# A larger head piece in a free strip buffer and a last group in three parts, in a DMA-bound diagonal prefix-sum kernel

## The chip, the cores and the metric

The kernel runs on one core of one Trainium2 chip. The metric is device time in microseconds (us), the median of several executions. All executions told here are of the fast state. A ratio is the mean time of one kernel's fast runs over the mean of the other's of the same rounds on the same chip, so it is not quite the ratio of the medians quoted beside it. Its 95% interval is given in brackets. Different sets of rounds ran on different chips.

## The reference

```python
def setup_inputs():
    B, H, W = 4, 4224, 4224
    return {"x": np.random.randn(B, H, W).astype(np.float32)}

def reference(x):
    ps = np.cumsum(np.cumsum(x, axis=1), axis=2)
    diag = np.diagonal(ps, axis1=1, axis2=2)
    return np.cumsum(diag, axis=1).astype(np.float32)
```

Every element of x has to be read once: 4 x 4224 x 4224 floats, 285 MB. The output is tiny.

## The kernel before: what the change touches

Rows are handled in groups of 384. Most of x is loaded in strips of 768 rows (6 rows on each of 128 partitions) by casting transfers, f32 to bf16, issued from GpSimd. There are three strip buffers. TensorE adds the columns right of the diagonal, VectorE (DVE) and ScalarE (ACT) the rows left of it. The last group of the last batch is loaded in pieces, so that little work is left when the last byte lands. A "head" of it, the last 528 columns of its first 256 rows, is loaded right at the start through the hardware queue in f32, while the casting queue gets going.

```python
    HC = 528
    src_a = x[LB, T0:TB, :].rearrange("(h p) w -> p h w", p=P)
    head = last.tile([P, 2, HC], FP32, name="head")
    nc.sync.dma_start(out=head, in_=src_a[:, :, N - HC : N])
    ...                                           # strips: pool "strips", bufs=NBUF (3)
    prefetched = []
    for i in range(NBUF):
        t = strip_tile()
        load_rows(t, 0, i * F2 * P)
        prefetched.append(t)
    ...                                           # batch loop; last batch only, after its last strips:
            part_a = strip[:, 0:2]                # 2 x 128 rows, without the head's columns
            part_b = strip[:, 2]                  # the last 128 rows
            acuts = [(1536, N - HC), (0, 1536)]
            bcuts = [(2432, TB), (640, 2432), (0, 640)]
            ...                                   # five casting transfers; first piece of a is folded here
        ...                                       # pu, carry, two scans (c12), output of the other groups
        fold_in(fold_a, part_a, c0, cp, 256)      # second piece of a
        ...
        row_sums(arows, asum)
        for i, ((c0, c1), (wp, wa)) in enumerate(zip(bcuts, shares)):
            fold_in(fold_b, part_b, c0, c0 + wp, 256, start=i == 0)
            ...
            if i == 0:
                matmul(fin_b, arows[:, 0:1], weights[:, 2 * P : GW], start=True)
                matmul(fin_b, arows[:, 1:2], weights[:, P : 2 * P])
                matmul(fin_a, arows[:, 0:1], weights[:, 0 : 2 * P], start=True)
                matmul(fin_a[:, P : 2 * P], arows[:, 1:2], weights[:, 0:P])
        row_sums(ttot, tsum)
        matmul(fin_b, ttot, weights[:, 0:P])
```

`fold_in` is a chain of matmuls with the identity that add columns of bf16 data into one bank of PSUM, the memory that TensorE writes to. The names that matter in the tail: `d` holds what each position of the diagonal adds, `pu` the sums of `d` by group, `arows` the row sums of part a (256 rows), `tsum` and `ttot` those of part b (128 rows). "The last add" is DVE's last instruction, which makes the last 128 results. I call the four products with `arows` "the fin products". In the program the fold of the middle piece of part b stands behind them, and in the trace it runs behind them (661.37, 661.80, then 662.64).

## Time and profile before

| | before |
|---|---|
| median of the first runs | 669.56 us (668.67 to 670.19) |
| span of the profiled execution | 667.0 us |
| casting queue, share of the 16 DMA engines' span | 99.7% |
| busiest compute engine | DVE, 50% |

A timeline line has the start and the length in us, the engine, the source line, the operation, output<-input, shape and count. What stands in brackets is the idle time ahead of it and what ended that. The lines themselves are shown in the prediction.

### The profile page before, as it was taken

Reading aid. Unit: us, or ns where it says so; the run is one execution under the profiler, and the core shown is the slowest. Engines: PE = TensorE matmul, PEld = TensorE weight load, DVE = VectorE, ACT = ScalarE, POOL = GpSimd, SP = SyncE. Lnnn points to the kernel's source line nnn. Section 1 sums busy time; section 2 is a strip of 40 time slices with the busy share of each in tenths; the row PEclk is TensorE's granted clock in tenths of the full one; section 3 lists DMA queues with packets and bytes.
Section 4 is the critical chain, followed back from the end, with each engine's and each line's share of the span. In section 5 each row is a group of like instructions: output and inputs, shape, how many; then the busy total and the mean of one; then the engine's idle time right before and its main releaser. Section 6 shows DMA issues by size and latency. Waiting matters only on the chain.

```text
span 667.0 us, 2828 instructions
## 1 busy us (share of the span) xinstructions
PE 215.1 (32%) x967; PEld 97.2 (15%) x967; DVE 336.3 (50%) x376; ACT 140.1 (21%) x225; POOL 27.0 (4%) x56
## 2 busy tenths in 40 slices
PE   0071522403118254140321633504032254250426
PEld 0030211101003022010110311201011122120202
DVE  2043617366924351745883415266398241635687
ACT  0001120406300103040630020304063002030436
POOL 5000000000000000000000000000000000001000
PEclk9995857666558586665655957567565586765758
DMA  9999999999999999999999999999999999999997
GB/s 203 219 219 219 218 219 219 217 217 216 208 215 219 219 219 217 216 219 219 219 219 215 216 211 217 220 219 216 216 216 219 220 215 218 216 215 219 216 207 144
DMA packets 7384, 143.25 MB, mean 215 GB/s; under 512 B 669, under 2 KB 842, under 8 KB 1866
## 3 DMA queue, kind: packets, MB, share of 16 engines
q0 software_dynamic: 7008, 142.47, 99.7%
q1 hardware_dynamic: 362, 0.61, 0.3%
q8 instruction: 7, 0.11, 0.1%
q14 instruction: 7, 0.06, 0.0%
HBM read 285.47 MB, written 0.07 MB: 428 GB/s over the span
## 4 chain that ended last, share of the span: by engine, by line
another core or an unknown queue 42%; DVE 25%; PE 23%; DMA 5%; issue 4%; DVEq 0%; POOLq 0%
PE d L198 23%; DVE acc L215 17%; DVE mu L218 7%; DMA strip<-in_x_dram 5%; PE fold L198 1%; DVE pu L215 0%; DVE c L397 0%; DVE c L218 0%; DVE tsum L215 0%; DVE acc L301 0%; DVE acc L304 0%; PE carry_ps L198 0%; DVE rows L331 0%; DVEq L218 0%
## 5 line engine op out<-in xcount | busy, mean ns | idle before, releaser
L218 DVE SCALAR_TENSOR_TENSOR mu<-strip,um 128x768 bf16<-128x768 bf16 (+1 forms) x129 | 110.7, 908 | 314.4 <-DMA strip<-in_x_dram 222.3
L198 PE MATMUL d<-strip,sel 128*11 128x384 bf16 x603 | 140.0, 406 | 344.4 <-DMA strip<-in_x_dram 344.4
L210 ACT ACTIVATE dump<-strip 128x416 bf16<-128x416 bf16 (+8 forms) x112 | 128.4, 1146 | 523.2 <-DMA strip<-in_x_dram 520.2
L215 DVE TENSOR_REDUCE acc<-strip 128x6 f32<-128x4608 bf16 (+6 forms) x23 | 195.9, 8518 | 0.0
L198 PEld LDWEIGHTS <-sel 128*11 128x11 bf16 x849 | 86.1, 101 | 526.3 <-issue 488.4
L198 PE MATMUL d<-mu,sel 128*11 128x384 bf16 x243 | 59.7, 355 | 67.5 <-DVE mu L218 67.4
L75 POOL DMA_DIRECT2D strip<-in_x_dram x24 | 16.5, 687 | 555.5 <-DVE acc L215 414.5
L210 ACT ACTIVATION_READ_ACCUMULATOR dump<-strip 128x1 f32 x112 | 20.9, 186 | 0.0
L218 DVE DVE_READ_ACCUMULATOR mu<-strip,um 128x1 f32 x129 | 10.6, 82 | 0.0
L198 PE MATMUL d<-ident,rows 128*11 128x128 f32 x24 | 5.2, 378 | 16.5 <-DVE rows L340 16.5
L198 PE MATMUL fold<-strip,ident_h 128*128 128x480 bf16 (+1 forms) x14 | 4.3, 458 | 8.4 <-DMA strip<-in_x_dram 8.4
L198 PE MATMUL d<-halves,rows 128*11 128x64 f32 x48 | 5.7, 304 | 0.0
L198 PEld LDWEIGHTS d<-halves,rows 128*11 128x11 f32 x48 | 5.1, 136 | 2.1 <-issue 2.1
L198 PEld LDWEIGHTS d<-ident,rows 128*11 128x11 f32 x24 | 2.6, 118 | 18.2 <-DVE rows L340 11.5
L215 DVE TENSOR_REDUCE pu<-d 11x1 f32<-11x384 f32 x4 | 2.2, 546 | 5.5 <-PE d L198 5.5
L397 DVE TENSOR_TENSOR_SCAN c<-ones_row,carry,c 11x384 f32<-11x384 f32 x4 | 4.0, 1006 | 0.1
L397 DVE TENSOR_TENSOR_SCAN c<-ones_row,carry,d 11x384 f32<-11x384 f32 x4 | 4.0, 1001 | 0.1
L198 PEld LDWEIGHTS <-ident_h 128*128 128x128 bf16 x20 | 2.2, 112 | 12.2 <-issue 11.8
L215 DVE TENSOR_REDUCE parts<-strip 128x3 f32<-128x3072 bf16 x1 | 3.4, 3350 | 0.0
L198 PE MATMUL d<-hmu,sel 128*11 128x384 bf16 (+2 forms) x3 | 0.7, 286 | 6.7 <-DVE hmu L218 6.7
L372 POOL DMA_DIRECT2D strip<-in_x_dram x2 | 1.4, 716 | 29.2 <-DVE acc L215 29.2
L215 DVE TENSOR_REDUCE tsum<-strip 128x1 f32<-128x384 bf16 (+2 forms) x3 | 1.7, 568 | 0.9 <-DMA strip<-in_x_dram 0.9
(78 smaller groups left out, 36.0 us busy)
## 6 DMA issues: line engine op xcount, KB each, us to landing
strip<-in_x_dram POOLq DMA_DIRECT2D x19, 6336.0 KB, 69.6
strip<-in_x_dram POOLq DMA_DIRECT2D x5, 3168.0 KB, 55.3
strip<-in_x_dram POOLq DMA_DIRECT2D x1, 1080.0 KB, 45.3
strip<-in_x_dram POOLq DMA_DIRECT2D x1, 768.0 KB, 48.2
head<-in_x_dram SPq DMA_DIRECT2D x1, 528.0 KB, 3.9
strip<-in_x_dram POOLq DMA_DIRECT2D x1, 448.0 KB, 51.1
strip<-in_x_dram POOLq DMA_DIRECT2D x1, 416.0 KB, 49.5
strip<-in_x_dram POOLq DMA_DIRECT2D x1, 160.0 KB, 51.4
```

The source lines that it names most:

```text
L75: nc.gpsimd.dma_start(out=o, in_=x[b, r0 : r0 + f * P, :].rearrange("(p f) w -> p f w", f=f))
L198: nc.tensor.matmul(o, lhsT=lhsT, rhs=rhs, start=start, stop=False, skip_group_check=True)
L210: nc.scalar.activation(out=dump[:, :w], in_=src, func=ACT.Copy, accum_out=acc)
L215: nc.vector.reduce_sum(out=acc, in_=src, axis=AX.X)
L218: nc.vector.scalar_tensor_tensor(out=o, in0=i, scalar=1.0, in1=m, op0=ALU.mult, op1=ALU.mult, accum_out=acc,)
L372: nc.gpsimd.dma_start(out=part_a[:, :, c0:c1], in_=src_a[:, :, c0:c1])
L397: nc.vector.tensor_tensor_scan(out=c12[:, i, :], data0=ones_row, data1=src, initial=carry[:, i : i + 1], op0=ALU.mult, op1=ALU.add,)
```

## The change

The intent, as the diff reads, is to load more of the last group early and in longer contiguous runs (8448 bytes), to put it into a strip buffer that is still free, and to leave less for the end, each part of 128 rows being handled by itself. The core of the diff:

```diff
-    HC = 528
-    src_a = x[LB, T0:TB, :].rearrange("(h p) w -> p h w", p=P)
-    head = last.tile([P, 2, HC], FP32, name="head")
-    nc.sync.dma_start(out=head, in_=src_a[:, :, N - HC : N])
+    HC = N // 2
+    HP2 = 2 * P
...
+    head = strips.tile([P, F, N], FP32, name="strip")[:, 0, :HC]
+    nc.sync.dma_start(out=head, in_=x[LB, T0 : T0 + P, N - HC : N])
     prefetched = []
-    for i in range(NBUF):
+    for i in range(NBUF - 1):
...
-                diag_b = last.tile([P, P], BF16, name="diag_b")
-                nc.gpsimd.dma_start(out=diag_b, in_=x[b, TB:N, TB:N])
+                ends = last.tile([P, 2, HP2], BF16, name="ends")
+                nc.gpsimd.dma_start(
+                    out=ends,
+                    in_=x[b, T0 + P : N, N - HP2 : N].rearrange("(h p) w -> p h w", p=P),
+                )
...
-            wp, ws = 1280, 1280 + 1536
+            wp, ws = 1440, 1440 + 1440
...
-            acuts = [(1536, N - HC), (0, 1536)]
-            bcuts = [(2432, TB), (640, 2432), (0, 640)]
+            apieces = [(0, 0, N - HC, 1024), (1, 1536, N - HP2, 1280), (1, 0, 1536, 768)]
+            bpieces = [(2176, N - HP2), (640, 2176), (0, 640)]
...                     # the fin products stay between the first and the second fold of part b
+        fold_in(fold_b, src, c0, c0 + 768, 256, start=True)
+        act_sum(tsum[:, 1:2], src[:, c0 + 768 : c1])
+        matmul(fin_b, arows[:, 0:1], weights[:, 2 * P : GW], start=True)
+        matmul(fin_b, arows[:, 1:2], weights[:, P : 2 * P])
+        matmul(fin_a, arows[:, 0:1], weights[:, 0 : 2 * P], start=True)
+        matmul(fin_a[:, P : 2 * P], arows[:, 1:2], weights[:, 0:P])
+        fold_in(fold_b, src, c2, c2 + 768, 256)
...
```

More of the change, by code (lines that the diff above doesn't have):

```diff
@@ L239 @@
         nc.vector.memset(rows3[i], 0.0)
-    asum = last.tile([P, 2, 5], FP32, name="asum")
-    tsum = last.tile([P, 8], FP32, name="tsum")
+    asum = last.tile([P, 2, 4], FP32, name="asum")
+    tsum = last.tile([P, 7], FP32, name="tsum")
     hs = last.tile([P, 3], FP32, name="hs")
@@ L246 @@
     hmu = last.tile([P, 3, GW], BF16, name="hmu")
-    row_sums(hs[:, 0:2], head)
-    for h in range(2):
-        w = GW - h * P
-        masked(hmu[:, h, :w], head[:, h, HC - w : HC], um1[:, :w], hu[:, h : h + 1])
-    nc.vector.tensor_sub(out=asum[:, :, 0], in0=hs[:, 0:2], in1=hu[:, 0:2])
+    row_sums(hs[:, 0:1], head)
+    masked(hmu[:, 0, :], head[:, HC - GW : HC], um1, hu[:, 0:1])
+    nc.vector.memset(asum, 0.0)
     for b in range(B):
@@ L315 @@
             if not whole and s == 0:
-                diag_b = last.tile([P, P], BF16, name="diag_b")
-                nc.gpsimd.dma_start(out=diag_b, in_=x[b, TB:N, TB:N])
-            if not whole and s == 1:
-                row_sums(hs[:, 2:3], diag_b)
-                masked(hmu[:, 2, :P], diag_b, um1[:, :P], hu[:, 2:3])
-                nc.vector.tensor_sub(
-                    out=tsum[:, 0:1], in0=hs[:, 2:3], in1=hu[:, 2:3]
-                )
+                ends = last.tile([P, 2, HP2], BF16, name="ends")
[3 more added lines that the diff above has]
+                )
+            if not whole and s == 1:
+                row_sums(hs[:, 1:3], ends)
+                for h in range(2):
+                    w = (2 - h) * P
+                    masked(
+                        hmu[:, h + 1, :w],
+                        ends[:, h, HP2 - w :],
+                        um1[:, :w],
+                        hu[:, h + 1 : h + 2],
+                    )
+                nc.vector.tensor_sub(out=asum[:, :, 0], in0=hs[:, 0:2], in1=hu[:, 0:2])
+                nc.vector.tensor_sub(out=tsum[:, 0:1], in0=hs[:, 2:3], in1=hu[:, 2:3])
                 for h in range(3):
@@ L365, with a_piece @@
         if not whole:
-            strip = strip_tile()
-            part_a = strip[:, 0:2]
-            part_b = strip[:, 2]
-            acuts = [(1536, N - HC), (0, 1536)]
-            for c0, c1 in acuts:
-                nc.gpsimd.dma_start(out=part_a[:, :, c0:c1], in_=src_a[:, :, c0:c1])
-            bcuts = [(2432, TB), (640, 2432), (0, 640)]
-            for c0, c1 in bcuts:
-                nc.gpsimd.dma_start(out=part_b[:, c0:c1], in_=x[b, TB:N, c0:c1])
-            fold_a = psum_s.tile([P, 2, 256], FP32, name="fold_a")
-            c0, c1 = acuts[0]
-            cp, ca = c0 + 768, c0 + 768 + 1152
-            fold_in(fold_a, part_a, c0, cp, 256, start=True)
-            for h in range(2):
-                act_sum(asum[:, h, 1:2], part_a[:, h, cp:ca])
-            row_sums(asum[:, :, 2], part_a[:, :, ca:c1])
+            parts_l = strip_tile()
+            apieces = [(0, 0, N - HC, 1024), (1, 1536, N - HP2, 1280), (1, 0, 1536, 768)]
+            for h, c0, c1, _ in apieces:
+                r0 = T0 + h * P
+                nc.gpsimd.dma_start(
+                    out=parts_l[:, h, c0:c1], in_=x[b, r0 : r0 + P, c0:c1]
+                )
+            bpieces = [(2176, N - HP2), (640, 2176), (0, 640)]
+            for c0, c1 in bpieces:
+                nc.gpsimd.dma_start(out=parts_l[:, 2, c0:c1], in_=x[b, TB:N, c0:c1])
+            fold_a = psum_s.tile([P, 2, 256], FP32, name="fold_a")
+            def a_piece(n, start):
+                h, c0, c1, wp = apieces[n]
+                src = parts_l[:, h]
+                fold_in(fold_a[:, h], src, c0, c0 + wp, 256, start=start)
+                act_sum(asum[:, h, 1 + n // 2 : 2 + n // 2], src[:, c0 + wp : c1])
+            a_piece(0, True)
         pu = smalls.tile([NG, 2], FP32, name="pu")
@@ L411 @@
             continue
-        c0, c1 = acuts[1]
-        cp = c0 + 768
-        fold_in(fold_a, part_a, c0, cp, 256)
-        for h in range(2):
-            act_sum(asum[:, h, 3:4], part_a[:, h, cp:c1])
-        row_sums(asum[:, :, 4], fold_a)
+        a_piece(1, False)
+        a_piece(2, False)
+        row_sums(asum[:, :, 3], fold_a)
         arows = last.tile([P, 2], FP32, name="arows")
@@ L426 @@
         fin_b = psum_s.tile([1, P], FP32, name="fin_b")
-        shares = [(768, 512), (768, 512), (0, 320)]
-        n = 1
-        for i, ((c0, c1), (wp, wa)) in enumerate(zip(bcuts, shares)):
-            fold_in(fold_b, part_b, c0, c0 + wp, 256, start=i == 0)
-            act_sum(tsum[:, n : n + 1], part_b[:, c0 + wp : c0 + wp + wa])
-            if i == 2:
-                row_sums(tsum[:, n + 2 : n + 3], fold_b)
-            row_sums(tsum[:, n + 1 : n + 2], part_b[:, c0 + wp + wa : c1])
-            n += 2
-            if i == 0:
-                matmul(fin_b, arows[:, 0:1], weights[:, 2 * P : GW], start=True)
-                matmul(fin_b, arows[:, 1:2], weights[:, P : 2 * P])
-                matmul(fin_a, arows[:, 0:1], weights[:, 0 : 2 * P], start=True)
-                matmul(fin_a[:, P : 2 * P], arows[:, 1:2], weights[:, 0:P])
+        src = parts_l[:, 2]
+        (c0, c1), (c2, c3), (c4, c5) = bpieces
+        fold_in(fold_b, src, c0, c0 + 768, 256, start=True)
[5 more added lines that the diff above has]
+        fold_in(fold_b, src, c2, c2 + 768, 256)
+        act_sum(tsum[:, 2:3], src[:, c2 + 768 : c2 + 768 + 384])
+        row_sums(tsum[:, 3:4], src[:, c2 + 768 + 384 : c3])
+        act_sum(tsum[:, 4:5], src[:, c4 : c4 + 320])
+        row_sums(tsum[:, 5:6], fold_b)
+        row_sums(tsum[:, 6:7], src[:, c4 + 320 : c5])
         ttot = last.tile([P, 1], FP32, name="ttot")
```

## The prediction

> **What bounds the kernel now.** I read the page first, then the chain of waits, then the timeline of the last 18 us by engine, because a kernel that is limited by one thing for 98% of its span can only be changed at its two ends.
>
> ```profile
> span 667.0 us, 2828 instructions
> PE 215.1 (32%) x967; PEld 97.2 (15%) x967; DVE 336.3 (50%) x376; ACT 140.1 (21%) x225; POOL 27.0 (4%) x56
> DMA  9999999999999999999999999999999999999997
> GB/s 203 219 219 219 218 219 219 217 217 216 208 215 219 219 219 217 216 219 219 219 219 215 216 211 217 220 219 216 216 216 219 220 215 218 216 215 219 216 207 144
> q0 software_dynamic: 7008, 142.47, 99.7%
> q1 hardware_dynamic: 362, 0.61, 0.3%
> ```
>
> The reader is to see that no compute engine is over 50% busy while the DMA row is 9 from the first slice to the last but one. The rate of 219 GB/s is counted where the bf16 values land; the source is f32, so 438 GB/s are read. Every element of x is read exactly once before and after the change, so the DMA floor (142.5 MB at 0.219 MB/us, about 651 us) does not move. 667 less 651 leaves about 16 us: the start, the slower small pieces, and the tail after the last byte. Full strips land every 29.89 us (64.5, 95.4, 125.3, 155.1 in the timeline of PE); each is issued over 50 us before it lands, so the DMA queue always holds the next one.
>
> The tail is where the change can matter. Timeline of the last 18 us, first TensorE without its weight loads, then VectorE:
>
> ```profile
> 649.63 3.36 PE L198 MATMUL fold<-strip,ident_h 128*128 128x480 bf16 x8 [7.21 <-DMA strip<-in_x_dram]
> 652.91 1.13 PE L198 MATMUL d<-strip,sel 128*11 128x384 bf16 x3
> 653.83 1.17 PE L198 MATMUL d<-mu,sel 128*11 128x384 bf16 x3
> 654.79 1.22 PE L198 MATMUL d<-halves,rows 128*11 128x64 f32 x12
> 655.85 0.82 PE L198 MATMUL d<-ident,rows 128*11 128x128 f32 x6
> 661.37 0.60 PE L198 MATMUL fin_b<-weights,arows 128*1 128x128 f32 x4 [0.39 <-DVE arows L215]
> 661.80 0.81 PE L198 MATMUL fin_a<-weights,arows 128*1 128x256 f32 x4
> 662.64 0.49 PE L198 MATMUL fold<-strip,ident_h 128*128 128x256 bf16 x3
> ```
> ```profile
> 651.12 3.35 DVE L215 TENSOR_REDUCE parts<-strip 128x3 f32<-128x3072 bf16 x1
> 655.21 0.17 DVE L215 TENSOR_REDUCE rows<-parts 128x3 f32<-128x12 f32 x1
> 656.71 0.55 DVE L215 TENSOR_REDUCE pu<-d 11x1 f32<-11x384 f32 x1 [0.78 <-PE d L198]
> 658.33 1.00 DVE L397 TENSOR_TENSOR_SCAN c<-ones_row,carry,d 11x384 f32<-11x384 f32 x1
> 659.37 1.01 DVE L397 TENSOR_TENSOR_SCAN c<-ones_row,carry,c 11x384 f32<-11x384 f32 x1
> 660.30 0.66 DVE L215 TENSOR_REDUCE asum<-fold_a 128x2 f32<-128x512 f32 x1
> 662.62 0.69 DVE L215 TENSOR_REDUCE tsum<-strip 128x1 f32<-128x512 bf16 x1 [0.94 <-DMA strip<-in_x_dram]
> 664.13 0.16 DVE L215 TENSOR_REDUCE ttot<-tsum 128x1 f32<-128x8 f32 x1
> ```
>
> Read it as one race. At 649.6 the last three-row strip lands and starts a serial compute chain: folds, column sums, d complete at 656.7, carry, two scans to 660.4, the sums of parts a, the fin products to 662.6. Meanwhile the five pieces of the last group land, the middle piece of part b at 662.6. The two arrive at the same moment: TensorE finishes its fin products at about 662.6 and its next fold, which needs the piece, starts at 662.64. So the compute chain has next to no slack against the DMA in this run. That is the central fact for what follows.
>
> **What the Trainium skill says.** "DMA: Bandwidth & Descriptors", section "Issuing engines are not separate DMA queues", says that transfers from all issuing engines interleave on the same 16 DMA engines. The trace agrees: the first strip, issued at 1.33 us, lands at 34.62, 33.3 us later, against a spacing of 29.89 between strips; the head's 0.54 MB at 438 GB/s is 1.24 us of the 3.4 us excess. The same page, "Anatomy of one DMA", gives a fixed cost of about 2.0 us for a transfer from this queue; 3.4 less 1.24 is 2.2, which fits. Its section "Why small descriptors are slow" puts the fixed part of a packet at a few cycles, important at 256 bytes and not at 2 KB; nothing in this trace separates the head's 2112-byte runs from 8448-byte ones. "TensorE: Matmul & The Clock Gate", section "What's actually happening", says that full clock is granted after one busy window of about 3.4 us of a free-running counter. The trace agrees: PE starts at 649.63 and the granted clock goes from 0.50 to 1.00 at about 655.6, 6 us later; after the start at 589.3 it does so at about 594.0, and at 619.2 about 624.8. The wait is therefore luck between 3.4 and 6.8 us, and this profile shows an unlucky tail.
>
> **The change, part by part.**
>
> Head: 2 x 128 x 528 = 135,168 elements become 128 x 2112 = 270,336, in f32 on the hardware queue. That adds 135,168 x 4 = 0.54 MB of reading at the start, 1.24 us at 438 GB/s. It is issued at the same time (about 0.8 us) and cannot start earlier, and the strips are ready to flow shortly after, so I take most of it as a delay of the strips: 1.0 to 1.24 us. DVE's row sum of it grows from 1.20 us (1056 elements) to about 2.3 and a masked product of 0.41 goes away; DVE is idle for 25.8 us before the first strip, so this costs nothing.
>
> Third buffer: the head occupies one of three strip buffers, so only two strips are prefetched ahead and the third is issued after the constants and the head's reduction, at about 11 us rather than 2.9. Two strips are about 60 us of transfer, so the queue holds work until about 64 us. Cost: none.
>
> Ends: the diagonal block of 128 x 128 becomes 2 x 128 x 256, 49,152 more elements, 0.098 MB, 0.45 us at 219 GB/s. The strip behind the diagonal block landed at 559.40, 30.09 after the one before it, 0.20 over the norm, for a quarter of that size, so 0.4 us more is right. DVE does about 0.7 us more at that point, beside a wait of 10 us: free.
>
> Tail pieces: before 552,960 + 393,216 + 524,288 = 1,470,464 elements, 2.94 MB, at the 213 GB/s of that stretch 13.8 us. After, six pieces with 1,286,144 elements, 2.57 MB, 12.1 us. The 1.7 us saved here are the 1.24 + 0.45 put in earlier. So the last byte lands when it did, within some 0.2 us, but the last three-row strip lands about 1.5 us later (649.6 becomes about 651.1). The change moves bytes from behind that strip to before it, and so takes time from the compute chain that starts there.
>
> That chain afterwards: folds 9 instead of 8 at 0.42 us (+0.4 on PE at half clock); the reduce of parts over 2880 rather than 3072 elements, -0.2 on DVE; ACT 1440 columns rather than 1536, -0.1 each; a reduce of asum (0.65) leaves DVE but lay in a gap. At the old, unlucky clock PE would have d ready 1.5 + 0.4 = 1.9 us later. With an average clock (full speed about 5.1 us after the start) the column sums and halves end sooner and DVE's rows become the limit: d is ready about 6.85 us after the strip, against 7.05 in this profile, so about 658.0 instead of 656.7: +1.3. From there carry, scans, the fold_a reduction, arows and fin products are unchanged in length (5.9 us), and the next fold of part b stands behind the fin products on PE. The landing of that piece no longer matters. Behind it, DVE's reduce of the middle piece is 384 instead of 512 (-0.15) but lies beside the fold; the last three reduces, ttot, fin_b, yl and the output keep their length. Sum: about +1.3 on the path, less about 0.2 for a head that fills some idle DMA time: +1.1 us. 669.56 + 1.1 is about 670.7.
>
> **Rivals.** First, the head is hidden after all: if the strips' first bytes need longer to begin than I think, and the 256 short runs of the old head were badly used, the larger head costs almost nothing and the whole stream ends up to 1.3 us earlier. For it: in windows of half a microsecond almost nothing moves before 2.0 us, and the rate is ragged until 6 us. Against it: first strip plus head already account for the 3.4 us. It would make 668.5 to 669.3. Second, a full clock loss: TensorE gets its full clock only after the column sums in most runs, and the chain is 2 us longer: 671.6. Third, the buffer: if the late third strip left the queue empty, a gap of many us would appear near 64 us; 50 us of margin speak against it, and I give it under 1%. Fourth, the tail is hidden: the chain in a typical run before has some 0.4 us of slack that this profile doesn't show, which makes 670.2.
>
> **Range and chances.** The centre is 670.7. The three runs of before span 1.5 us, the clock's luck up to 2 us, the head's overlap 1.2 us; 8 times in 10 I expect 669.0 to 672.3. Two per cent is 13 us, far more than any term here: same 0.98, faster 0.01, slower 0.01.
>
> **What would show each step.** The first strip's first matmul near 35.8 instead of 34.64 shows that the head delays the strips; at 34.7 the first rival holds. Spacing of 29.9 us for the strips after it, with no gap near 64, clears the buffer. The first fold near 651.1 shows the shift, and the strip behind the ends landing about 0.4 us later than the usual spacing shows their part. In the tail, pu should start near 658, and the wait of 0.94 us for DMA before the reduce of the middle piece should vanish, with TensorE's fold of it behind the fin products: that is compute as the bound. If instead DVE still waits there for the DMA and the span is shorter, I was wrong about which of the two runners is the later.

## The result, and the profile after

The changed kernel took 671.29 us (671.12 to 671.76, 6 runs) against 669.67 us for the kernel before in the same rounds. The ratio is 1.0027 [1.0014, 1.0040]: 1.6 us slower, clear of the noise, and within 2%. A second set of rounds gave 670.85 against 669.00, ratio 1.0019 [1.0004, 1.0033].

From the page of the changed kernel:

```profile
span 669.8 us, 2842 instructions
GB/s 230 216 215 207 217 216 217 218 218 218 218 220 218 216 218 218 216 217 218 218 218 217 216 213 218 217 218 218 213 216 215 220 218 217 218 216 218 215 208 109
q1 hardware_dynamic: 234, 1.15, 0.5%
```

The stream of the DMA is the same in the middle. The first slice moved more bytes than before (the head is f32 in both memories and twice as large), and the last slice less: 109 GB/s against 144, because the span goes on longer after the bytes are in.

The tail of the changed kernel, TensorE without its weight loads, then DVE:

```profile
651.56 3.72 PE L199 MATMUL fold<-strip,ident_h 128*128 128x480 bf16 x9 [8.41 <-DMA strip<-in_x_dram]
657.16 0.83 PE L199 MATMUL d<-ident,rows 128*11 128x128 f32 x6
662.68 1.01 PE L199 MATMUL fin_b<-weights,arows 128*1 128x128 f32 x4 [1.18 <-DVE arows L216]
663.49 1.48 PE L199 MATMUL fin_a<-weights,arows 128*1 128x256 f32 x4
664.91 0.82 PE L199 MATMUL fold<-strip,ident_h 128*128 128x256 bf16 x3
```
```profile
656.94 0.17 DVE L216 TENSOR_REDUCE rows<-parts 128x3 f32<-128x12 f32 x1
658.03 0.55 DVE L216 TENSOR_REDUCE pu<-d 11x1 f32<-11x384 f32 x1 [0.92 <-PE d L199]
662.85 0.55 DVE L216 TENSOR_REDUCE tsum<-strip 128x1 f32<-128x384 bf16 x1 [0.31 <-DMA strip<-in_x_dram]
665.76 0.42 DVE L216 TENSOR_REDUCE tsum<-fold 128x1 f32<-128x256 f32 x1 [2.36 <-PE fold L199]
666.69 0.16 DVE L216 TENSOR_REDUCE ttot<-tsum 128x1 f32<-128x7 f32 x1
```

The last three-row strip lands 1.93 us later (651.56 against 649.63), and pu starts 1.32 us later (658.03 against 656.71). The middle piece of part b lands almost when it did (DVE takes it at 662.85 against 662.62), so the stream as a whole is not late. DVE used to wait 0.94 us for that piece. Now it waits 0.31 us for it, and then 2.36 us for TensorE's fold of it, which stands behind the fin products. The last add ends at 667.80 against 665.05.

There is a second thing to see. The fin products and the fold have grown, although they are the same instructions. The mean granted clock tells why. First the kernel before, then the changed one, in two stretches of the tail (stretch, its length, busy us and count of PE, PEld, DVE, ACT and POOL, then granted clock, DMA share and GB/s):

```profile
661.50:662.50 1.00, 1.00 (x8) 0.48 (x6) 0.18 (x1) 0.00 (x0) 0.00 (x0) 1.00 0.40 71
662.50:665.50 3.00, 0.98 (x7) 0.37 (x5) 2.17 (x6) 1.28 (x4) 0.00 (x0) 1.00 0.02 3
```
```profile
661.50:662.50 1.00, 0.00 (x1) 0.00 (x0) 0.90 (x3) 0.70 (x2) 0.00 (x0) 0.72 0.41 73
662.50:665.50 3.00, 2.82 (x11) 1.15 (x11) 0.59 (x2) 1.18 (x4) 0.00 (x0) 0.50 0.04 7
```

Before, TensorE is busy with the fin products in the first stretch and keeps 1.00. In the changed kernel arows comes later, TensorE stands still there, and the clock falls to 0.50 (at 661.94) just before its longest serial stretch begins.

The difference of the two last adds, 2.75 us, splits cleanly: pu comes 1.32 later; from pu to arows it is 4.35 us (656.71 to 661.06) and 4.34 us (658.03 to 662.37); from arows to the last add it is 3.99 us and 5.43 us, 1.44 more. These two profiled executions took 668.75 and 671.53 us, further apart than the medians. The second profiles of the two kernels (below) split otherwise: the last adds end at 666.24 and 667.77, 1.53 us apart; pu comes 1.57 later (656.67 and 658.24), and from arows to the last add it is 5.23 and 5.18 us, because there the kernel before lost the clock too. So the later pu is in both pairs, and the 1.44 us of the clock in one of two.

### The profile page after: what moved, and what is told of

Same layout as the page of the kernel before. It is cut to its first block, busy times and chain, and to the rows that moved or that the text cites. A ratio compares the mean times of both kernels' runs of the same rounds, so it can differ in the third digit from the quotient of the medians.

```text
span 669.8 us, 2842 instructions
## 1 busy us (share of the span) xinstructions
PE 216.0 (32%) x974; PEld 98.3 (15%) x974; DVE 336.6 (50%) x375; ACT 139.2 (21%) x223; POOL 26.9 (4%) x57
## 4 chain that ended last, share of the span: by engine, by line
another core or an unknown queue 41%; DVE 27%; PE 23%; DMA 5%; issue 4%; DVEq 0%; POOLq 0%
PE d L199 22%; DVE acc L216 17%; DVE mu L219 7%; DMA strip<-in_x_dram 5%; DVE parts L216 1%; DVE pu L216 0%; DVE c L408 0%; DVE c L219 0%; PE fin_b L199 0%; DVE acc L303 0%; DVE acc L300 0%; PE fin_a L199 0%; PE carry_ps L199 0%; DVE rows L340 0%
## 5 line engine op out<-in xcount | busy, mean ns | idle before, releaser
L216 DVE TENSOR_REDUCE parts<-strip 128x3 f32<-128x2880 bf16 x1 | 3.1, 3150 | 0.0
L216 DVE TENSOR_REDUCE hs<-strip 128x1 f32<-128x2112 f32 x1 | 2.4, 2353 | 0.1
```

Source lines behind the costliest of these rows:

```text
L216: nc.vector.reduce_sum(out=acc, in_=src, axis=AX.X)
```

## The experiments

My theory was that bytes moved ahead of the last strip delay a serial chain that had no slack, and that the clock adds to it. The rivals were that the lost buffer costs, that the handling in three parts costs by itself, that the form of the head's load matters, or that the last byte still sets the end. The landing of the last three-row strip (the start of TensorE's first fold of the tail) is my measure of the stream, and "arows to the last add" my measure of the end of the chain.

**1. The buffer alone.** The kernel before, with its old head in a strip buffer:

```diff
-    head = last.tile([P, 2, HC], FP32, name="head")
+    head_t = strips.tile([P, F, N], FP32, name="strip")
+    head = head_t[:, 0:2, :HC]
-    for i in range(NBUF):
+    for i in range(NBUF - 1):
```

> The kernel before with one part of the change alone: its old head (2 x 128 rows x 528 columns) now lies in the third strip buffer, so the third strip is issued late. Theory (bytes ahead of the last strip delay the serial chain of the tail): nothing changes, within 0.4 us of before, first strip lands at 34.6, the strip behind it about 29.9 later, no gap near 64 us. Rival (the lost prefetch buffer costs): 0.5 us or more slower than before, with a longer spacing around the third strip.

It took 669.58 us, ratio 0.9990 [0.9975, 1.0004]. The third strip was issued at 10.04 us and landed at 95.63, with a spacing of 29.88 from the one before; the last strip landed at 649.87. No cost of the buffer shows. The first strip, however, landed at 35.86 rather than at 34.6 with the same head: my number for it missed, and the landing of the first strip is a poor measure.

**2. The bytes of the head, with the tail of before.** As 1, and

```diff
-    HC = 528
+    HC = 1056
-            cp, ca = c0 + 768, c0 + 768 + 1152
+            cp, ca = c0 + 768, c0 + 768 + 624
```

> As the first, and the head has as many bytes as in the changed kernel (2 x 128 rows x 1056 columns, 4224-byte runs), the tail of the kernel before otherwise kept. Theory: the first strip lands 1.2 to 1.4 us later than before (about 35.9), the last three-row strip about 1.3 later (650.9), the last byte at the same time as before; the sums for d are ready about 1.0 later and the time rises by 0.6 to 1.2 us. Rival (the new handling of the last group in three parts costs, not the head): within 0.3 us of before. Second rival (8448-byte runs matter): the first strip here lands clearly later than the 35.99 of the changed kernel.

It took 670.78 us, ratio 1.0008 [0.9992, 1.0024]: the interval holds no change as well as the expected loss, so by time this is inconclusive. The profile is clearer:

```profile
651.28 3.13 PE L200 MATMUL fold<-strip,ident_h 128*128 128x480 bf16 x8 [7.11 <-DMA strip<-in_x_dram]
657.08 0.83 PE L200 MATMUL d<-ident,rows 128*11 128x128 f32 x6 [0.93 <-DVE rows L217]
```

The last strip landed 1.41 us later than in experiment 1, which differs by nothing but the head's size and the shares that follow from it; I had reckoned 1.24 for the 0.54 MB. TensorE then waits for DVE's rows, the limit that the prediction named. The clock stayed at 1.00 to the end here, and the last add came at 666.16, 0.87 later than in experiment 1 (665.29). That understates it a little: experiment 1's tail ran at a granted clock of 0.75 from about 653.1 us on, and the first profile of before, at 1.00, had its last add at 665.05.

**3. Half the head in the changed kernel, twice.**

```diff
-    HC = N // 2
+    HC = N // 4
-apieces = [(0, 0, N - HC, 1024), ...
+apieces = [(0, 0, N - HC, 2048), ...
```

> The changed kernel with half the head (128 rows x 1056 columns, as many bytes as the head before; the first part of the last group takes over the other columns, 1024 more of them on TensorE). Theory: first strip at about 34.7, last three-row strip about 650.4, everything in the tail chain about 1.2 us earlier, time 0.8 to 1.6 us below the changed kernel, so within about 0.7 us of before. Rival (three-part handling itself costs): stays within 0.3 us of the changed kernel, 1.6 above before.

It took 671.26 us, ratio 1.0017 [1.0001, 1.0033], and the last strip landed at 651.84 instead of the expected 650.4. This was a clear miss, so I ran it again beside the changed kernel itself.

> The half-head version of the changed kernel once more, because its first profile had the first strip at 37.19 and the third at 96.98, some 1.5 us later than its bytes explain, and its times spread over 2 us. Theory: that was a late stream in some executions; this time the third strip lands near 95.4 to 95.7 (as before and the buffer-only run), the last three-row strip at 650.2 to 650.8, and the time is 0.5 us or more below the changed kernel of this call. Rival: the small head in one row per partition has a cost of its own; third strip again near 97, time equal to the changed kernel within 0.3 us.

> The changed kernel unaltered, as the partner of the other three on the same chip: 671.0 to 671.7 us, first strip at 36.0, third strip near 96.5, last three-row strip near 651.5; TensorE's granted clock falls back to 0.50 before the fin products, as in its first profile.

The half head took 671.04 us, ratio 1.0023 [1.0008, 1.0038]; the changed kernel 670.85 us, ratio 1.0019. The last strip landed at 651.86 with the half head and at 651.69 with the whole one. So giving half of the bytes back does not bring the stream forward, and my theory of bytes alone does not hold for the half head. It came late in both profiles, which speaks against chance.

The whole stream is late here, and in the changed kernel it is not. All kernels load the same bytes in all, and the same 640 columns of part b remain behind its middle piece, so DVE's reduce of that piece, where it waits for the DMA, shows how late the stream as a whole is. The half head (repeat), then the changed kernel (second profile):

```profile
664.36 0.55 DVE L216 TENSOR_REDUCE tsum<-strip 128x1 f32<-128x384 bf16 x1 [1.37 <-DMA strip<-in_x_dram]
```
```profile
662.97 0.55 DVE L216 TENSOR_REDUCE tsum<-strip 128x1 f32<-128x384 bf16 x1 [0.23 <-DMA strip<-in_x_dram]
```

The half head reads 664.38, 664.36 and (experiment 5) 664.60, the changed kernel 662.85, 662.97 and (experiment 6) 662.74, the old head 662.62, 662.98, 662.86 and (experiment 8) 662.65. Nor does the half head lose it all at its own load: in each of its three profiles one strip between 156 and 263 us comes about 1.1 us late (30.97 us behind the one before it, 231.54 to 262.51, in the first), long after the head has landed. So the half head has a delay that the whole head does not show, and the half head can't serve as the changed kernel with fewer bytes.

This also means that the run cannot isolate the three-part handling, which I had meant it to do; that part was not run alone, and its own cost, if any, stays open.

**4. The form of the head's load alone.** The kernel before, with the same 0.54 MB into the same tile, but from 128 rows of x:

```diff
-    nc.sync.dma_start(out=head, in_=src_a[:, :, N - HC : N])
+    nc.sync.dma_start(
+        out=head.rearrange("p h w -> p (h w)"), in_=x[LB, T0 : T0 + P, N - 2 * HC : N]
+    )
```

> The kernel before with the form of the head's load alone changed: the same 0.54 MB into the same tile, but as 128 runs of 4224 bytes instead of 256 of 2112 (other elements of x, so the last group's result is wrong on purpose). Form theory (128 longer runs in one row per partition make the first strips late, as the half-head version suggests): third strip at 96.5 to 97.0, 1.1 or more later than before, time 0.4 to 1.2 us above before. Bytes theory: third strip at 95.4 to 95.7, time as before within 0.3.

> The kernel before, unaltered, for a second profile of its start. Expected as the first: first strip 34.6 to 35.9 (a pause of about 0.9 us fell into the third strip in one profile and into the first in the buffer-only run), third strip 95.3 to 95.7, ratio to before 1.000 within its interval.

This loads other elements, so some results are wrong (the comparison's tolerance let them pass). It took 670.42 us, ratio 1.0009 [0.9993, 1.0025], against 669.27 us, ratio 0.9993 [0.9978, 1.0007], for the unaltered kernel before in the same rounds. The means are 670.44 and 669.35. In the profile:

```profile
651.22 3.36 PE L200 MATMUL fold<-strip,ident_h 128*128 128x480 bf16 x8 [6.95 <-DMA strip<-in_x_dram]
```

In four profiles of programs with the old head's form and size this strip landed at 649.63, 650.00, 649.87 and 649.66. Here it landed 1.2 to 1.6 us later with no byte more (and the middle piece of part b at 664.21). In this one profile that is as much as doubling the bytes in experiment 2. That the form does it is not shown: 1.1 us of it is one late strip (the third, 30.98 us behind the second), and by time the interval holds no change.

The second profile of before also landed its first strip at 36.52 and its third at 96.43 (34.64 and 95.37 in the first), yet its last at 650.00. The first profile had later extra waits that the second had not (30.82 instead of 29.9 us between its second and third strip on TensorE, and 15.48 instead of 14.95 near the end). The landing of the last strip repeats better: to 0.4 us in the four profiles with the old head (649.63 to 650.00), and to 0.25 us in the five with the changed one (651.44 to 651.69).

**5. The half head in two transfers.** As 3, but

```diff
+    for c in range(0, HC, 528):
+        nc.sync.dma_start(
+            out=head[:, c : c + 528],
+            in_=x[LB, T0 : T0 + P, N - HC + c : N - HC + c + 528],
+        )
```

> The half-head version of the changed kernel with that head loaded by two transfers of 528 columns, so again 256 runs of 2112 bytes, result right. Form theory: third strip back at 95.4 to 95.8, last three-row strip at 650.3 to 650.8, time 0.7 to 1.3 us below the 671.04 of the half head. If neither form nor bytes are the cause (something in the changed program's start makes its strips late): third strip still at 96.5 to 97.0 and no gain.

It took 671.18 us, ratio 1.0018 [1.0001, 1.0035], and

```profile
652.05 3.75 PE L203 MATMUL fold<-strip,ident_h 128*128 128x480 bf16 x9 [7.38 <-DMA strip<-in_x_dram]
```

The runs of 2112 bytes are back, and the stream is as late as ever. So the length of the runs alone does not explain it; that the second transfer has a cost of its own was not tested. Of "the form" it is left that 128 rows of x are read instead of 256, or which columns. Neither explains all runs: the changed kernel's own head reads 128 rows too, and the columns of experiment 3 are those of experiment 2, and in these two the end of the stream is not late (in experiment 2 the first piece of part b landed at 660.89, with the old head at 660.49 to 660.86). I leave the cause open.

**6. Holding the clock.** The changed kernel with spare matmuls in TensorE's idle stretches, written to a bank that nobody reads:

```diff
+            def keep_busy(n, src, c):
+                for i in range(n):
+                    matmul(spare, ident_h, src[:, c : c + 512], start=True)
...
         a_piece(2, False)
+        keep_busy(2, parts_l[:, 1], 0)
...
+        keep_busy(4, src, c0)
         matmul(fin_b, arows[:, 0:1], weights[:, 2 * P : GW], start=True)
```

> The changed kernel with six spare matmuls (512 columns, into a bank nobody reads) put in TensorE's two idle stretches of the tail, two before the fold of the first piece of part b and four before the fin products; the result is unchanged. Theory of the clock: the granted clock stays at 1.00 until the end, fin products take 1.3 us together instead of 2.3 and the fold behind them 0.49 instead of 0.82, the last fin 0.4 instead of 0.6; time 1.0 to 1.6 us below the changed kernel. Rival (the clock falls anyway or the later strip alone makes the loss): no more than 0.3 us gained, or a loss of up to 1 us from the added matmuls.

It took 670.16 us, ratio 1.0001 [0.9987, 1.0015]. The tail on TensorE, and the clock in the last stretch:

```profile
662.57 0.60 PE L199 MATMUL fin_b<-weights,arows 128*1 128x128 f32 x4 [0.31 <-DVE arows L216]
663.00 0.81 PE L199 MATMUL fin_a<-weights,arows 128*1 128x256 f32 x4
663.75 0.50 PE L199 MATMUL fold<-strip,ident_h 128*128 128x256 bf16 x3
```
```profile
662.50:665.50 3.00, 1.76 (x12) 0.91 (x13) 1.67 (x5) 1.18 (x4) 0.00 (x0) 1.00 0.02 4
```

The strip landed at 651.44 and pu started at 657.91, as in the changed kernel. The clock stayed at 1.00, the products took what they took before, and arows to the last add fell from 5.43 to 3.86 us. The median is 1.1 us below the changed kernel's first one, as expected; they are not of the same rounds, so the strength of this is in the profile. Work that computes nothing made this tail faster.

What takes the clock can be read from the profiles afterwards; no run was made for it. In the tails, as in the first profiles of both kernels from the first rise on, the clock stays at 1.00 for whole multiples of 3.41 us (655.11 to 661.94 in the changed kernel, two of them; 655.60 to 665.84 before, three). Without spare matmuls it fell ahead of the last add in all six profiles of the new tail, in one of the five of the old. In the tails it fell after a stretch of 3.41 us with 1.72 us or less of matmuls, and stayed after one with 1.80 or more:

| profile | stretch | TensorE busy, us of 3.41 | clock after it |
|---|---|---|---|
| before, first | 659.01 to 662.43 | 1.84 | 1.00 |
| before, second | 657.75 to 661.17 | 1.36 | 0.50 |
| changed, first | 658.52 to 661.94 | 1.72 | 0.50 |
| changed, second | 659.56 to 662.98 | 1.63 | 0.50 |
| experiment 2 | 660.87 to 664.29 | 2.17 | 1.00 |
| experiment 6 | 659.04 to 662.46 | 3.00 | 1.00 |

The boundary is not sharp: one stretch with 1.85 us, near 435 us in the changed kernel's first profile, was followed by 0.50. So an idle stretch of a given length does not decide it: experiment 2 waits 1.22 us ahead of its fin products, the changed kernel 1.18, and only the latter lost the clock. The share of such a stretch that is busy seems to decide, and where the stretch begins is chance.

**7. TensorE's order.** The changed kernel with the two fin_a products behind the fold of the middle piece; alone, and then together with 6:

```diff
-        matmul(fin_a, arows[:, 0:1], weights[:, 0 : 2 * P], start=True)
-        matmul(fin_a[:, P : 2 * P], arows[:, 1:2], weights[:, 0:P])
         fold_in(fold_b, src, c2, c2 + 768, 256)
+        matmul(fin_a, arows[:, 0:1], weights[:, 0 : 2 * P], start=True)
+        matmul(fin_a[:, P : 2 * P], arows[:, 1:2], weights[:, 0:P])
```

> The changed kernel with the fin_a products moved behind the fold of the middle piece of part b on TensorE (fin_b stays ahead of it). Theory (the tail is bound by TensorE's serial order behind arows): the fold ends 0.7 to 1.4 us earlier, DVE's reduce of it too, the last fin then waits for fin_a; time 0.4 to 1.0 us below the changed kernel. Rival (the DMA's last piece sets the end): no change within 0.2 us.

> Both remedies: spare matmuls to hold the clock, and the fin_a products behind the fold. Theory: 0.3 to 0.6 us below the spare matmuls alone (670.16), so 669.5 to 669.9, equal to the kernel before within 0.3 us, since the last byte lands at the same time in both; no version of the tail gets below that by more than 0.5 us.

In the same rounds as the second run of the changed kernel (mean 670.69), the order alone had a median of 670.12 and a mean of 669.93, ratio to before 1.0006 [0.9992, 1.0020]; both remedies 669.61 and 669.65, ratio 1.0003 [0.9991, 1.0015]. With the order alone:

```profile
663.46 0.60 PE L199 MATMUL fin_b<-weights,arows 128*1 128x128 f32 x4 [1.95 <-DVE arows L216]
663.99 0.58 PE L199 MATMUL fold<-strip,ident_h 128*128 128x256 bf16 x3
664.50 1.44 PE L199 MATMUL fin_a<-weights,arows 128*1 128x256 f32 x4
```

In this profile the full clock came late (near 657.5), so pu started at 658.81, 0.78 later than in the first profile of the changed kernel. Still the last add ended at 666.68, 1.12 earlier: arows to the last add took 3.52 us. Part of that is the order, since the fold no longer waits behind fin_a, and part the clock, which in this profile fell only at 664.29. With both remedies it took 3.21 us; against experiment 6 (3.86), both at 1.00, the order alone is worth 0.65 us. The last byte did not set the end in the changed kernel. Both remedies together take the median 1.2 us below the changed kernel of the same rounds and leave it even with the kernel before.

**8. The same spare matmuls in the kernel before.** The second profile of before had shown its own loss of the clock:

```profile
662.13 1.49 PE L198 MATMUL fin_a<-weights,arows 128*1 128x256 f32 x4
663.55 0.82 PE L198 MATMUL fold<-strip,ident_h 128*128 128x256 bf16 x3
```

That is 0.68 and 0.33 us longer than in the first profile, the clock having fallen at 661.17 (the expectation says 661.4), and the last add ended at 666.24 instead of 665.05. So I added four spare matmuls behind the second fold of part a and one ahead of the fin products.

```diff
         fold_in(fold_a, part_a, c0, cp, 256)
+        keep_busy(4, part_a[:, 0], 0)
...
             if i == 0:
+                keep_busy(1, part_b, c0)
                 matmul(fin_b, arows[:, 0:1], weights[:, 2 * P : GW], start=True)
```

> The kernel before with spare matmuls in its own tail: four behind the second fold of part a, one behind the first fold of part b. In the second profile of before the granted clock fell to 0.50 at 661.4 and the fold of the middle piece ended 0.7 later than DVE needed it; in the first it did not fall. Theory (that fall is what spreads the times of before from 668.7 to 671): the clock stays at 1.00 to the end, the reduce of the middle piece again waits for the DMA and not for TensorE, the median falls by 0.3 to 0.8 us below before of the same rounds, with few runs above 669.5, and this beats both kernels. Rival (the spread is in the stream of the DMA, which arrives up to 1 us later in some executions): no gain, ratio 0.999 to 1.001.

It took 669.00 us against 669.86, ratio 0.9996 [0.9981, 1.0011]. In its profile the clock stayed at 1.00, and of DVE's two waits, 1.34 us for the DMA and 0.74 for the fold of the middle piece, only the first was left (1.35 us). Four of its six runs lie between 668.79 and 669.06, but two at 670.7 and 670.8. It is not shown to be faster than the kernel before. If the clock held in these two as well, which the one profile cannot show, its loss is not all of that kernel's spread: the stream too may come late in some executions of the old head.

## Why the prediction was right or wrong

**The time.** 670.7 was predicted and 671.29 measured, inside the range of 669.0 to 672.3; the sign was right and the size, +1.1, was short of the measured +1.6. The 0.2 us that I took off for a head that fills idle DMA time did not show: pu came 1.3 and 1.6 us later in the two pairs of profiles, against the +1.3 before that deduction.

**The bound and the missing slack.** Right. A middle piece that lands at nearly the same time, a chain that comes later, and DVE waiting for TensorE instead of the DMA are what the profile after shows. Experiments 6 and 7 shorten only that chain and get the time back. I wrote that DVE's wait for the DMA should vanish; it shrank from 0.94 to 0.31 us, ahead of the new wait of 2.36.

**The third buffer and the ends.** Both right. Experiment 1 shows no cost of the buffer. The strip behind the ends came 30.58 us after the one ahead of it, against 30.09 for the smaller block before, 0.49 more; I had 0.45, worked from bytes. The 0.4 that I drew from the smaller block does not follow: 0.20 us for a quarter of the size would make 0.6 more. On TensorE, before and after:

```profile
529.31 10.60 PE L198 MATMUL d<-strip,sel 128*11 128x384 bf16 x54 [13.48 <-DMA strip<-in_x_dram]
559.40 8.96 PE L198 MATMUL d<-strip,sel 128*11 128x384 bf16 x42 [15.87 <-DMA strip<-in_x_dram]
```
```profile
530.75 11.32 PE L199 MATMUL d<-strip,sel 128*11 128x384 bf16 x54 [13.48 <-DMA strip<-in_x_dram]
561.33 9.45 PE L199 MATMUL d<-strip,sel 128*11 128x384 bf16 x42 [15.62 <-DMA strip<-in_x_dram]
```

**The head.** The sum came out; that the bytes are its reason fits and is not shown. I took 1.0 to 1.24 us for 0.54 MB more, and 0.45 for the ends. The last strip landed at 651.58 on average in the five profiles with the changed head and ends and at 649.79 in the four with the old ones: 1.79 us, where the bytes give 1.69, and the end of the stream did not move. With two rows per partition, doubling the bytes cost 1.41 us (experiment 2, one profile). But a head of 128 rows with the old bytes came 1.2 to 1.6 us late too (4), and giving back half of the changed head returned nothing (3, 5). Single late strips of up to 1.1 us, in the kernel before as well, are as large as the term that I wanted to see. I also dismissed the form too early, saying that nothing in the trace separates the two: nothing did, which was a reason for a trial and not for a zero. And the sign I named for it, the first strip at 35.8, is worthless: it read 35.99, but the unaltered kernel before read 36.52 in its second profile. There the excess that I took for 1.24 us of head and 2.0 us of fixed cost is 5.3 us instead of 3.4, so the agreement was that of one profile. I also listed 64.5 and 95.4 among strips that land every 29.89 us, although they are 30.8 apart.

**The strip and pu.** 651.1 and 658.0 were predicted, 651.56 and 658.03 measured. The strip came later than I thought and its chain was shorter (6.47 us rather than 6.85), since the clock rose early in that execution and DVE's rows became the limit, as I had said they would on average. The two errors cancel, which is luck. The luck of the clock's rise I put at 3.4 to 6.8 us; in the thirteen profiles that show the rise it came 2.8 to 6.0 us after the strip.

**The step that failed**, in the first pair of profiles, is "From there carry, scans, the fold_a reduction, arows and fin products are unchanged in length (5.9 us)". From pu to arows it held to 0.01 us. The fin products did not hold: from 662.68 to 664.97 they took 2.29 us instead of 1.24 (661.37 to 662.61), the fold behind them 0.82 instead of 0.49 and the last product 0.59 instead of 0.38, for the clock had fallen. I had the clock's luck as a rival, but put it at the column sums and thought only of when it rises. That the later chain took the clock is likely (six of six new tails lost it, one of five old ones), and spare matmuls held it in all three profiles that have them (6, 7, 8). It is no rule: the kernel before lost the clock in its second profile without any later chain.

## What to carry to other kernels

Where a kernel is bound by its DMA stream, as here, shifting bytes from the end to the start leaves the last byte where it was (662.85 and 662.97 against 662.62 and 662.98) and takes time from whatever waits for the last large tile; ask first which of the two runners of the tail is later. An idle stretch on TensorE ahead of a serial tail can cost more than its own length, if what follows runs at half the clock; look at the granted clock in short stretches, and consider useful work or spare matmuls there. Trust the landmark that repeats from profile to profile (here the last strip's landing), and take a second profile of the unaltered kernel before reading 1 us into any single one.

## What the Trainium skill lacked or had wrong

- "TensorE: Matmul & The Clock Gate", section "What's actually happening", gives the return to the half clock after an idle window of about 3.4 us. In the changed kernel the clock fell near 661.9 though TensorE had been busy for 1.74 us of the 3.5 between 658.5 and 662.0, and its gaps were 0.66 and 0.61 us and a last one that was some 0.4 us old by then (timeline of TensorE). Partial idleness sufficed: in the tails of these runs the clock was lost after 3.41 us with up to 1.72 us of matmuls and kept after 1.80 or more.
- No page that I found accounts for the late streams of the kernels that load 0.54 MB from 128 rows (middle piece of part b at 664.21 to 664.60 in experiments 3 to 5, against 662.62 to 662.98 with the old head). "DMA: Bandwidth & Descriptors", section "Why small descriptors are slow", speaks of the descriptors' size, which alone does not explain it: with runs of 2112 bytes from 128 rows (experiment 5) the last strip still landed at 652.05.
- No page that I found mentions that an otherwise even stream (29.89 us from strip to strip) has single late strips: 30.98 between the second and third in experiment 4, 30.82 in the first profile of the kernel before, 30.6 in the changed kernel, none there in experiment 1.
